# One low part per unit on GpSimd, a fourth raw buffer, and seven of eight groups with seven products

## The chip, the cores and the metric

The kernel runs on one core of a Trainium2 chip. The metric is the device time of one execution in microseconds (us); lower is better. TensorE (PE) multiplies, VectorE (DVE), ScalarE (ACT) and GpSimd (POOL) work on elements, SyncE (SP) issues the weight loads. Weights lie in HBM, tiles in SBUF, matmul results in the eight banks of PSUM.

## The reference

One decoder layer on 256 tokens of width 2048, in float32:

```
h = x + 0.5 * swiglu(rms_norm(x, g1), w_gate1, w_up1, w_down1)      # D_FF = 5632
h = h + mixer(rms_norm(h, gm))                                      # two groups of attention heads
y = h + 0.5 * swiglu(rms_norm(h, g2), w_gate2, w_up2, w_down2)
swiglu(x, g, u, d) = (silu(x @ g) * (x @ u)) @ d
```

The change concerns the two SwiGLU layers (FFN 1 up to about 705 us of the execution, FFN 2 from about 1044 us); the mixer between them is left as it is.

## The kernel before

**Products.** Every float32 weight tile is split into a high part (`hi`, rounded for TensorE, made by ACT from the loaded `raw` tile) and a low part (`lo` = `raw` - `hi`, a DVE subtraction of two SBUF tiles, called a low below; `low`, L440). One product (`product`, `mm3`) is three matmuls of 128 x 128 by 128 x 512: high by high, high by low, low by high.

**Groups.** A group is one 1 MB weight load: 128 partitions by four tiles of 512 columns, a 2 x 2 block of weight tiles against a 2 x 2 block of activation tiles (two halves of the contraction, two halves of the tokens). A group of kind `D` (`whole`, L443) does the eight products of a plain block product: one load, one ACT cast of 2048 columns, one low of 2048 columns. A group of kind `S` (`seven`, L480) does the same block with seven products in the manner of Winograd's form of Strassen's method. DVE first makes four sums of weight tiles (`outer`, L499: two at once; `inner`, L506 and L507: one after the other) in a `sums` tile, and then needs two lows, one of 1536 columns for the plain tiles and one of 2048 for the sums. The sums of the activation tiles (`form_of`, the tiles `fu`) are made once for each pair of contraction tiles, the first time that pair is used in an `S` group.

**Units.** A unit (`unit`) is 512 columns of gate and 512 of up, with eight groups, one for each pair of contraction tiles; `UNITS` gives the kind of each. An FFN has 11 units. When the last `S` group has ended, its banks `Q0` to `Q3`, which are common to the unit, are folded into the four results by eight DVE operations, the steps (`step`, L699): each reads one PSUM bank and one SBUF tile. Two SiLUs on ACT and two DVE multiplications (L722, the `s` tile, called f below) follow, then eight transposes on PE (L571) and their split into `hT` (again PSUM against SBUF). The down projection of unit b - 1, four `D` groups (`down`, `DOWN`), stands behind unit b's groups; the last two units' downs end the FFN.

**Order.** Nothing here is ordered by dependencies at run time alone: `arrange` walks through all tasks of an FFN with a cost for each (`cast`, `sub`, `LOADS`, a due place in PE's sequence, buffers taken and given back) and writes one fixed order for each engine. Every engine then works through its own list, waiting on semaphores. Buffers are counted in `NRAW` (loaded tiles), `NSUM`, `NHI` and `NLO`: 3, 2, 5 and 5. All weight loads are issued from the one SP queue, in the order of the groups.

Of the kernel before, what the change touches and what calls it, by code (L numbers as in the profile page):

```python
# [9 lines left out]
F32 = mybir.dt.float32  # L10
# [7 lines left out]
P = 128  # L18
# [77 lines left out]

class Task:
    def __init__(self, eng, cost, run, need=(), due=0, take=(), give=(), lag=LAG, rows=False, moves=0):
        self.moves, self.seeds = moves, None
        self.eng, self.cost, self.run, self.need, self.due = eng, cost, run, list(need), due  # L100
        self.take, self.give, self.lag, self.rows = dict(take), list(give), lag, rows
        self.got, self.end, self.then = {}, None, []


def arrange(tasks, pools):
# [19 lines left out]
    dirty = set(pools["bank"])  # L125
    queues, seen = {"sp": [], "pool": []}, [0.0]
# [30 lines left out]

    def open_(t):
        if t.seeds is not None and (takers[t.seeds] > takers[pos] or all(b in dirty for b in free["bank"])):
            return False  # L160
        return all(len(free[r]) >= k and (r not in lines or lines[r][0] is t) for r, k in t.take.items())
# [90 lines left out]
def hybrid_layer(ctx: ExitStack, tc: tile.TileContext, a: dict, out: bass.AP):  # L252
# [124 lines left out]
    def mm3(o, shi, slo, mhi, mlo, start, stop, seeded=False):  # L377
        nc.tensor.matmul(o, lhsT=shi, rhs=mhi, start=start, stop=False, skip_group_check=seeded)  # L378
        nc.tensor.matmul(o, lhsT=shi, rhs=mlo, start=False, stop=False, skip_group_check=seeded)  # L379
        nc.tensor.matmul(o, lhsT=slo, rhs=mhi, start=False, stop=stop, skip_group_check=seeded)  # L380
# [29 lines left out]
    def ffn(pool, u, wgu, wd, slots, banks, rstd, held=None, first=None, lead=None, done=None, out=None):  # L410
# [15 lines left out]
        def own(tag, i, shape, dt):  # L426
            if (tag, i) not in made:
                made[tag, i] = (sp if tag == "sqh" else pool).tile(shape, dt, tag=tag, name=tag, bufs={"s": 1}.get(tag, 2))
            return made[tag, i]
# [10 lines left out]
        def low(o_, a, b):  # L440
            tt(out=o_, in0=a, in1=f32(b), op=ALU.subtract)  # L441

        def whole(src, pieces):  # L443

            n, new, by = 2048 // pieces, [], []
            for j in range(pieces):
                m = slice(j * n, j * n + n)
                ld = task("sp", 0.06, None, take={"raw": 1} if j == 0 else (), lag=0, moves=1 / pieces)
                c = task("act", cast(n), None, [ld], take={"hi": 1} if j == 0 else ())
                l = task("dve", sub(n), None, [c], take={"lo": 1} if j == 0 else ())  # L450
# [7 lines left out]
                ld.run = lambda raw=raw, m=m: nc.sync.dma_start(raw(), src[:, m])  # L458
                c.run = lambda raw=raw, hi=hi: nc.scalar.copy(hi(), raw())  # L459
                l.run = lambda raw=raw, hi=hi, lo=lo: low(lo(), raw(), hi())  # L460
# [19 lines left out]
        def seven(src):  # L480
# [5 lines left out]
            b = task("dve", 2 * sub(512), None, [a])  # L486
# [17 lines left out]
            def inner():  # L504
                s, r = cols_of(sm()), cols_of(raw())
                tt(out=s[2], in0=s[0], in1=r[2], op=ALU.add)  # L506
                tt(out=s[3], in0=s[2], in1=r[1], op=ALU.add)  # L507

            a.run, b.run = outer, inner
            w = [([c, l], lambda i=i: (cols_of(hi())[i], cols_of(lo())[i])) for i in range(3)]  # L510
            w += [([cb, ls], lambda i=i: (cols_of(hs())[i], cols_of(lt())[i])) for i in range(4)]
            new = [(ld, -30), (c, 0), (a, 0), (l, 0)] + [(t, 3) for t in (ca, b, cb, ls)]
            return new, w, {2: [("hi", c), ("lo", l)], 6: [("hi", ca), ("lo", ls)]}

        def product(held, key, stat, w, need):
# [9 lines left out]
            def run():  # L525
                mm3(bank_of(b), *stat(), *w[1](), start=b["first"] is t, stop=b["last"] is t, seeded="seed" in b)
# [5 lines left out]
        def group(kind, src, held, stat, need, form=None, pieces=1, last=False):  # L532

            new, w, free = seven(src) if kind == "S" else added_low(src) if kind == "L" else whole(src, pieces)
# [46 lines left out]
        def into_u(un, gcol, due):  # L581

            def finish(k, v, x):
                ends = []
                for j in range(2):
# [4 lines left out]
                    ), [c] + ends[-1:], due)  # L590
# [33 lines left out]
        def form_of(p, need, due):  # L624

            tile_, over = fu[seven_of.index(p)], u(2 * p)[:, :, P:SEQ]
# [17 lines left out]
            def round_():  # L644
                x = views(a)[1]
                nc.scalar.copy(tile_[:, :, 0, :], x[:, :3])
                nc.scalar.copy(over[:, 0, :], x[:, 3])

            def left():
                x = views(a)[1]  # L650
                low(tile_[:, :, 1, :], x[:, :3], tile_[:, :, 0, :])
# [5 lines left out]
            at = lambda i: (tile_[:, i, 0, :], tile_[:, i, 1, :]) if i < 3 else (over[:, 0, :], over[:, 1, :])  # L657
# [4 lines left out]
        def unit(b):  # L662
# [29 lines left out]
            if ns:  # L692
# [4 lines left out]
                def step(o_, key, in1, op, need, due, free=True):  # L697
                    return task(
                        "dve", 0.605, lambda: tt(out=o_(), in0=bank_of(held[key]), in1=in1(), op=op), need + [held[key]["last"]], due,  # L699
                        give=[("bank", held[key]["first"])] if free else (),  # L700
                    )

                s0, s1 = lambda: s_tile()[:, 0, :], lambda: s_tile()[:, 1, :]
                d1 = step(x, "Q2", s0, ALU.add, [q], due)
                d2 = step(y, "Q1", x, ALU.subtract, [d1], due, False)
                d3 = step(s1, "Q3", x, ALU.add, [d1], due)
                d4 = step(x, "Q1", s1, ALU.subtract, [d2, d3], due)
                up = (y, x)
                g = [step(s0, (0, 0), s0, ALU.add, [d1], due + 1), step(s1, (1, 0), s1, ALU.add, [d3, d4], due + 4)]
                v = [step(y, (0, 1), y, ALU.add, [d2], due + 1), step(x, (1, 1), x, ALU.add, [d4], due + 5)]  # L710
            ends = []
            for t in range(NT):
# [8 lines left out]
                src = up[t] if ns else (lambda t=t: bank_of(R(t, 1)))  # L721
                f = task("dve", 0.66, lambda t=t, src=src: stt(  # L722
                    out=s_tile()[:, t, :], in0=src(), scalar=half_rms()[:, t : t + 1], in1=s_tile()[:, t, :], op0=ALU.mult, op1=ALU.mult,
                ), [a, v[t] if ns else R(t, 1)["last"]], due + 9 if ns else due + 2 * t, lag=1.5)
                if not ns:
                    f.give.append(("bank", R(t, 1)["first"]))
# [5 lines left out]
            def finish(k, v, x):  # L732
# [6 lines left out]
                l = task("dve", 0.605, lambda: low(rows_tile()[:, :, 1, :], v(), rows_tile()[:, :, 0, :]), [c], due + 4)  # L739
# [10 lines left out]
        rm_need, row_ready, row_of, row_split, moved = [], {}, {}, {}, {}  # L750

        def down(blocks, final):
# [5 lines left out]
            for i, (cp, b, c) in enumerate(todo):  # L758
# [4 lines left out]
                if not held[cp] and not final:  # L763
# [7 lines left out]
                    lambda k, b=b, c=c: row_ready[b, c], last=final_of_cp,  # L771
                )
# [11 lines left out]
        def settle(cp, held, final, later):  # L784

            due, ends = len(main), []
            for t in range(NT):
                for j in range(2):
                    tail = out is not None and cp == 1 and (t, j) == (1, 1)
                    for n, (a0, w) in enumerate(((0, 256), (256, 256)) if tail else ((0, 512),)):  # L790
# [11 lines left out]
                        x = task(*(("dve", sub(w)) if final else ("act", cast(w))), run, [held[t, j]["last"], *([moved[cp, t, j]] if final else [])], due + t + 4 * j, lag=0.6)  # L802
# [556 lines left out]
    with tc.tile_pool(name="f2", bufs=1, reuse_waits=REUSE) as fp:  # L1359
        slots, fu = [[], [], [], []], []  # L1360
        for i, nm, dt in F2_ORDER:
            if i == 4:
                fu += [fp.tile([P, 3, 2, P], F32R, name="fu%d" % p) for p in range(max(k.count("S") for k in UNITS[1]))]
            else:
                slots[i].append(fp.tile([P, 2048], dt, name="%s%d" % (nm, len(slots[i]))))
# [4 lines left out]
            lead={"residual": last_quarter, "next": (u2, ss2, V_G2), "forms": fu}, out=out.rearrange("(t p) d -> p t d", p=P),  # L1370
# [83 lines left out]
```

## Time and profile before

| what | value |
| --- | --- |
| time, median of 3 runs | 1744.66 us (1744.55 to 1745.9) |
| the profiled execution's own time | 1746.08 us |
| its span, first to last instruction | 1744.3 us |
| PE busy in the span | 1733.2 us (99%) |
| DVE busy | 1530.9 us (88%) |
| ACT busy | 1133.9 us (65%) |
| POOL busy | 11.5 us (1%) |
| granted TensorE clock | 1.00 |

A row of a timeline gives the start in us, the length in us, the engine, the line, the operation and its tiles, and in brackets the idle time of that engine ahead of it with what ended it. Operations of one engine overlap a little at their ends, so the time that one costs its engine is the distance from its start to the next one's. A row of busy times by stretches gives the stretch, its length, and for each engine the busy time and (x) the instructions.

### The profile page before, as it was taken

The numbers are of one execution on the slowest core, as the hardware profiler recorded it, in microseconds if no ns is written. First come the engines' busy times: TensorE is split into PE (matmuls) and PEld (weight loads), VectorE is DVE, ScalarE is ACT, GpSimd is POOL, SyncE is SP. The second block draws the span as 40 slices with busy tenths as digits, with TensorE's granted clock in tenths as the row PEclk, the third lists the DMA queues.
The fourth block names the chain that finished last, engine by engine and source line by source line (L and its number), as shares of the span: only waits on it lengthen the run. The fifth ranks groups of instructions, "written<-read, shape, count | busy, mean of one in ns | idle before, by whom it ended". The sixth has DMA issues, their size and how long they took to land.

```text
span 1744.3 us, 21098 instructions
## 1 busy us (share of the span) xinstructions
PE 1733.2 (99%) x8037; PEld 1440.2 (83%) x8037; DVE 1530.9 (88%) x1662; ACT 1133.9 (65%) x1380; POOL 11.5 (1%) x22
## 2 busy tenths in 40 slices
PE   9999999999999999999999999999999999999999
PEld 6888888888888888998788888888888888888887
DVE  7999999999999996668777769999999999999993
ACT  7677667767766764555766556667767766766761
POOL 0000000000000000000000000000000000000000
PEclk9999999999999999999999999999999999999999
DMA  8556556555545554564444456545555545555552
GB/s 340 197 206 224 201 185 217 196 190 217 216 175 212 217 208 154 157 206 158 133 146 144 133 185 249 181 181 219 192 193 217 210 178 216 217 202 185 218 195 118
DMA packets 62917, 339.73 MB, mean 195 GB/s; under 512 B 6752, under 2 KB 15456, under 8 KB 29280
## 3 DMA queue, kind: packets, MB, share of 16 engines
q1 hardware_dynamic: 62208, 337.18, 54.0%
q8 instruction: 63, 1.03, 0.2%
q0 software_dynamic: 320, 1.05, 0.1%
q14 instruction: 38, 0.31, 0.1%
q10 hardware_dynamic: 288, 0.16, 0.0%
HBM read 336.27 MB, written 2.10 MB: 194 GB/s over the span
## 4 chain that ended last, share of the span: by engine, by line
PE 95%; DVE 2%; ACT 1%; DMA 1%; issue 0%; SPq 0%; DVEq 0%; ACTq 0%
PE acc L379 24%; PE acc L378 24%; PE acc L380 24%; PE sm L378 6%; PE sm L379 6%; PE sm L380 6%; PE acc L571 1%; DVE wloy L441 1%; PE sm L1097 1%; PE sc L1286 1%; DMA rawx<-in_wgu 1%; PE sm L1103 1%; PE sm L1265 0%; DMA rawy<-in_wd 0%; DVE wlo L441 0%
## 5 line engine op out<-in xcount | busy, mean ns | idle before, releaser
L378 PE MATMUL acc<-whi,u 128*128 128x512 f32 (+1 forms) x671 | 256.1, 383 | 0.9 <-DVE s L1061 0.9
L379 PE MATMUL acc<-wlo,u 128*128 128x512 f32 (+1 forms) x671 | 256.2, 382 | 0.7 <-DVE wlo L441 0.6
L380 PE MATMUL acc<-whi,u 128*128 128x512 f32 (+1 forms) x671 | 254.7, 381 | 0.0
L295 DVE TENSOR_TENSOR wlo<-raw,whi 128x1024 fp32r<-128x1024 f32 (+1 forms) x112 | 128.8, 1154 | 70.4 <-ACT whi L294 69.8
L294 ACT CAST whi<-raw 128x1024 fp32r<-128x1024 f32 (+1 forms) x112 | 111.0, 991 | 93.2 <-PE acc L380 84.8
L441 DVE TENSOR_TENSOR wlo<-raw,whi 128x1536 fp32r<-128x1536 f32 (+3 forms) x76 | 146.7, 1934 | 6.6 <-ACT whi L459 6.5
L378 PEld LDWEIGHTS acc<-whi,u 128*128 128x128 f32 x671 | 125.9, 188 | 23.4 <-DVE s L1061 1.3
L379 PEld LDWEIGHTS acc<-wlo,u 128*128 128x128 f32 x671 | 126.0, 188 | 23.1 <-DVE wlo L441 2.0
L380 PEld LDWEIGHTS acc<-whi,u 128*128 128x128 f32 x671 | 125.8, 188 | 21.3 <-issue 0.8
L441 DVE TENSOR_TENSOR wlo<-sums,whi 128x2048 fp32r<-128x2048 f32 x46 | 105.1, 2285 | 16.2 <-ACT whi L487 16.2
L441 DVE TENSOR_TENSOR wlox<-raw,whix 128x2048 fp32r<-128x2048 f32 (+1 forms) x52 | 109.9, 2120 | 2.5 <-ACT whix L459 2.5
L441 DVE TENSOR_TENSOR wloy<-raw,whiy 128x1536 fp32r<-128x1536 f32 (+1 forms) x52 | 104.4, 2008 | 5.6 <-ACT whiy L459 5.5
L795 ACT COPY h<-acc 128x512 f32<-128x512 f32 (+1 forms) x117 | 64.1, 557 | 67.8 <-PE acc L380 67.4
L441 DVE TENSOR_TENSOR wloy<-sums,whiy 128x2048 fp32r<-128x2048 f32 x37 | 84.6, 2286 | 11.9 <-ACT whiy L487 11.9
L499 DVE TENSOR_TENSOR sums<-raw 128x1024 f32<-128x1024 f32 x77 | 93.6, 1217 | 0.0
L441 DVE TENSOR_TENSOR wlox<-sums,whix 128x2048 fp32r<-128x2048 f32 x34 | 77.7, 2285 | 13.7 <-ACT whix L487 13.7
L378 PE MATMUL acc<-whi,hT 128*128 128x512 f32 x224 | 88.5, 395 | 0.0
L379 PE MATMUL acc<-wlo,hT 128*128 128x512 f32 x224 | 87.3, 390 | 0.0
L380 PE MATMUL acc<-whi,hT 128*128 128x512 f32 x224 | 87.2, 389 | 0.0
L379 PE MATMUL acc<-wlox,u 128*128 128x512 f32 x216 | 84.2, 390 | 0.6 <-DVE wlox L441 0.6
L459 ACT CAST whi<-raw 128x2048 fp32r<-128x2048 f32 (+2 forms) x42 | 73.2, 1747 | 17.5 <-DMA raw<-in_wd 11.2
L378 PE MATMUL acc<-whix,u 128*128 128x512 f32 x216 | 84.1, 389 | 0.0
(341 smaller groups left out, 4558.0 us busy)
## 6 DMA issues: line engine op xcount, KB each, us to landing
raw<-in_wgu SPq DMA_DIRECT2D x109, 1024.0 KB, 4.8
raw<-in_wd SPq DMA_DIRECT2D x65, 1024.0 KB, 4.9
rawy<-in_wgu SPq DMA_DIRECT2D x33, 1024.0 KB, 4.7
rawx<-in_wgu SPq DMA_DIRECT2D x32, 1024.0 KB, 5.0
raw<-in_wf SPq DMA_DIRECT2D x48, 512.0 KB, 3.6
raw<-in_wo SPq DMA_DIRECT2D x32, 512.0 KB, 3.3
raw<-in_ws SPq DMA_DIRECT2D x32, 388.0 KB, 3.5
rawx<-in_wd SPq DMA_DIRECT2D x12, 1024.0 KB, 4.8
```

Source lines behind the costliest of these rows:

```text
L294: nc.scalar.copy(hi, src)
L295: nc.vector.tensor_tensor(out=lo, in0=src, in1=hi.bitcast(F32), op=ALU.subtract)
L378: nc.tensor.matmul(o, lhsT=shi, rhs=mhi, start=start, stop=False, skip_group_check=seeded)
L379: nc.tensor.matmul(o, lhsT=shi, rhs=mlo, start=False, stop=False, skip_group_check=seeded)
L380: nc.tensor.matmul(o, lhsT=slo, rhs=mhi, start=False, stop=stop, skip_group_check=seeded)
L441: tt(out=o_, in0=a, in1=f32(b), op=ALU.subtract)
L459: c.run = lambda raw=raw, hi=hi: nc.scalar.copy(hi(), raw())
L499: tt(out=sm()[:, :1024].rearrange("p (j n) -> p j n", j=2), in0=v[:, 0:3:2, :], in1=v[:, 3:4, :].broadcast_to([P, 2, 512]), op=ALU.add,)
L571: nc.tensor.transpose(bt[:, j * SEQ + t * P : j * SEQ + (t + 1) * P], src()[:, t, m], ident)
L795: nc.scalar.copy(o_, src)
L1097: nc.tensor.transpose(bt[:, j * P : (j + 1) * P], src[:, j, :], ident)
L1103: nc.tensor.matmul(bo[rows, c0 : c0 + SEQ], lhsT=vals(0, j), rhs=p0[:, j, :], start=True, stop=False)
```

## The change

- `UNITS`: from the fourth unit on, `SDSSSSSD` becomes `SSSSSSSD`, in eight units of each FFN.
- `BESIDE`, `AT_Q2`, `low`, `whole`, `slow`: of each down that isn't the FFN's last, the second of its four groups gets its low from GpSimd instead of DVE. The GpSimd instruction is tied by a semaphore to the matmul that ends bank `Q2` of the unit in front, the same matmul that the first step waits for.
- `Task.pair`, `shared`: the planner doesn't put a DVE task without a PSUM operand and a GpSimd task into the same time.
- `step`: the two steps that make the up results write into the PSUM bank that they read, and f reads that bank; so f too reads one PSUM and one SBUF tile, and frees the bank.
- `NRAW` 3 to 4; to make room, `s` and `fu` tiles, `PAD` and `SCRATCH` (the memory set aside for descriptors of GpSimd's DMAs) are re-arranged or cut.
- `inner` becomes two tasks, so that other work can stand between L506 and L507 (now both L538).
- The rule for the copies of `h` into PSUM banks ahead of a down (`open_`, `seeds`) counts free banks.

```diff
-UNITS = [["D" * 8, x, "DSSSSSSD"] + ["SDSSSSSD"] * (NB - 3) for x in ("DDSSDSSD", "DSSDSSSD")]
+UNITS = [["D" * 8, x, "DSSSSSSD"] + ["SSSSSSSD"] * (NB - 3) for x in ("DDSSDSSD", "DSSDSSSD")]
 DOWN = "DDDD"
+BESIDE = (1,)
+AT_Q2 = True
-NRAW, NSUM, NHI, NLO = 3, 2, 5, 5
-SCRATCH = 2048
+NRAW = 4
+SCRATCH = 512
...
+def slow(n):
+    return 0.4 + 0.0021 * n
...
+    def shared(t):
+        x = doing.get({"dve": "pool", "pool": "dve"}.get(t.eng))
+        return t.pair and x is not None and x.pair and x.end is not None and x.end > now + 1e-9
...
-        def low(o_, a, b):
-            tt(out=o_, in0=a, in1=f32(b), op=ALU.subtract)
+        def low(o_, a, b, behind=None):
+            if behind is None:
+                tt(out=o_, in0=a, in1=f32(b), op=ALU.subtract)
+                return
+            x = nc.gpsimd.tensor_tensor(out=o_, in0=a, in1=f32(b), op=ALU.subtract)
+            tc.add_manual_dep(x.ins, behind.made.ins.name, ...
...
-            b = task("dve", 2 * sub(512), None, [a])
+            b0 = task("dve", sub(512), None, [a])
+            b = task("dve", sub(512), None, [b0])
...
-                v = [step(y, (0, 1), y, ALU.add, [d2], due + 1), step(x, (1, 1), x, ALU.add, [d4], due + 5)]
+                up = [lambda t=t: bank_of(held[t, 1]) for t in range(NT)]
+                v = [step(up[0], (0, 1), y, ALU.add, [d2], due + 1, False), step(up[1], (1, 1), x, ALU.add, [d4], due + 5, False)]
...
+                    behind=beside.get(b + 1) if not final and i in BESIDE else None,
```

**DVE at the end of a unit.** The rows are from the middle of FFN 1, from the last lows ahead of the steps to the second f. `wlo`, `wlox` are low tiles, `whi`, `whix` high tiles, `raw`, `rawx` loaded ones; `sqh` and `s` hold the folded results, `acc` and `sm` are PSUM banks. Before:

```order
L441 TENSOR_TENSOR wlo_75<-raw_70,whi_73 128x2048
L441 TENSOR_TENSOR wlox_93<-raw_71,whix_90 128x2048
L441 TENSOR_TENSOR wlox_94<-rawx_87,whix_91 128x2048
L699 TENSOR_TENSOR sqh<-sm,s 128x512
L699 TENSOR_TENSOR sqh<-acc,sqh 128x512
L699 TENSOR_TENSOR s<-sm,sqh 128x512
L699 TENSOR_TENSOR s<-acc,s 128x512
L699 TENSOR_TENSOR sqh<-acc,s 128x512
L699 TENSOR_TENSOR sqh<-acc,sqh 128x512
L699 TENSOR_TENSOR s<-acc,s 128x512
L722 SCALAR_TENSOR_TENSOR s<-sqh,rmh,s 128x512
L699 TENSOR_TENSOR sqh<-acc,sqh 128x512
```

Now, in the same place:

```order
L464 TENSOR_TENSOR wlox_95<-rawx_88,whix_92 128x2048
L464 TENSOR_TENSOR wlox_96<-raw_70,whix_93 128x2048
L733 TENSOR_TENSOR sqh<-acc,s 128x512
L733 TENSOR_TENSOR sqh<-acc,sqh 128x512
L733 TENSOR_TENSOR s<-sm,sqh 128x512
L733 TENSOR_TENSOR s<-acc,s 128x512
L733 TENSOR_TENSOR sqh<-acc,s 128x512
L733 TENSOR_TENSOR acc<-acc,sqh 128x512
L757 SCALAR_TENSOR_TENSOR s<-acc,rmh,s 128x512
L733 TENSOR_TENSOR s<-acc,s 128x512
L464 TENSOR_TENSOR wlo_75<-rawx_87,whi_73 128x2048
L733 TENSOR_TENSOR acc<-acc,sqh 128x512
```

One low fewer stands ahead of the steps (that of the second down group, now on GpSimd), the first eight operations from the first step on all read PSUM, and the first operation with two SBUF inputs (`wlo_75`) comes behind them; a second such low and the second f come next.

**DVE at the beginning of a unit's groups**, with the splits of the first group, still in FFN 1. Before, behind the `hT` splits, an `S` group's sums, a `D` group's low (`wlox_94<-raw_70`) and the next `S` group:

```order
L499 TENSOR_TENSOR sums_89<-raw_71 128x1024
L506 TENSOR_TENSOR sums_89<-sums_89,raw_71 128x512
L507 TENSOR_TENSOR sums_89<-sums_89,raw_71 128x512
L441 TENSOR_TENSOR wlox_94<-raw_70,whix_91 128x2048
L499 TENSOR_TENSOR sums_88<-rawx_87 128x1024
L506 TENSOR_TENSOR sums_88<-sums_88,rawx_87 128x512
L507 TENSOR_TENSOR sums_88<-sums_88,rawx_87 128x512
L441 TENSOR_TENSOR wlox_95<-raw_71,whix_92 128x1536
```

Now, from the second f on:

```order
L531 TENSOR_TENSOR sums_89<-raw_70 128x1024
L531 TENSOR_TENSOR sums_90<-raw_71 128x1024
L538 TENSOR_TENSOR sums_89<-sums_89,raw_70 128x512
L538 TENSOR_TENSOR sums_90<-sums_90,raw_71 128x512
L464 TENSOR_TENSOR hT<-acc,hT 128x2x256
L538 TENSOR_TENSOR sums_89<-sums_89,raw_70 128x512
L464 TENSOR_TENSOR hT<-acc,hT 128x2x256
L464 TENSOR_TENSOR wlox_95<-raw_70,whix_92 128x1536
L464 TENSOR_TENSOR wlox_96<-sums_89,whix_93 128x2048
L538 TENSOR_TENSOR sums_90<-sums_90,raw_71 128x512
```

The `D` group has gone from among the `S` groups, and the sums of two groups are made with other work between their single steps.

**GpSimd in FFN 1**, where it had nothing before the mixer; these are the first of nine such rows (FFN 2 has nine more):

```order
L466 ISA
L466 TENSOR_TENSOR wlo_75<-raw_71,whi_73 128x2048
L466 TENSOR_TENSOR wlox_96<-raw_71,whix_93 128x2048
L466 TENSOR_TENSOR wlox_95<-raw_71,whix_92 128x2048
L466 TENSOR_TENSOR wlox_94<-raw_71,whix_91 128x2048
```

All nine read `raw_71`, so that buffer's next load waits for GpSimd and no longer for DVE.

More of the change, by code (lines that the diff above doesn't have):

```diff
@@ L94, in sub, with __init__ @@
     return 0.07 + 0.00104 * n
+def slow(n):
+    return 0.4 + 0.0021 * n
 class Task:
-    def __init__(self, eng, cost, run, need=(), due=0, take=(), give=(), lag=LAG, rows=False, moves=0):
+    def __init__(self, eng, cost, run, need=(), due=0, take=(), give=(), lag=LAG, rows=False, moves=0, psum=False):
         self.moves, self.seeds = moves, None
+        self.pair = (eng == "dve" and not psum) or (eng == "pool" and not moves)
         self.eng, self.cost, self.run, self.need, self.due = eng, cost, run, list(need), due
@@ L156, in since @@
         return max([x.end + x.lag for x in t.need], default=0.0)
+    def shared(t):
+        x = doing.get({"dve": "pool", "pool": "dve"}.get(t.eng))
+        return t.pair and x is not None and x.pair and x.end is not None and x.end > now + 1e-9
     def open_(t):
-        if t.seeds is not None and (takers[t.seeds] > takers[pos] or all(b in dirty for b in free["bank"])):
+        if shared(t):
             return False
+        if t.seeds is not None:
+            left = len(free["bank"]) - (takers[t.seeds] - takers[pos])
+            if left < 1 or sum(b not in dirty for b in free["bank"]) < 1:
+                return False
         return all(len(free[r]) >= k and (r not in lines or lines[r][0] is t) for r, k in t.take.items())
@@ L449, in whole @@
                 c = task("act", cast(n), None, [ld], take={"hi": 1} if j == 0 else ())
-                l = task("dve", sub(n), None, [c], take={"lo": 1} if j == 0 else ())
+                l = task(*(("dve", sub(n)) if behind is None else ("pool", slow(n))), None, [c], take={"lo": 1} if j == 0 else ())
+                if behind is not None:
+                    l.need.append(behind)
                 if j == 0:
@@ L459, in whole @@
                 c.run = lambda raw=raw, hi=hi: nc.scalar.copy(hi(), raw())
-                l.run = lambda raw=raw, hi=hi, lo=lo: low(lo(), raw(), hi())
+                l.run = lambda raw=raw, hi=hi, lo=lo: low(lo(), raw(), hi(), behind)
                 new += [(ld, -30), (c, 0), (l, 0)]
@@ L525, in run @@
             def run():
-                mm3(bank_of(b), *stat(), *w[1](), start=b["first"] is t, stop=b["last"] is t, seeded="seed" in b)
+                t.made = mm3(bank_of(b), *stat(), *w[1](), start=b["first"] is t, stop=b["last"] is t, seeded="seed" in b)
             t.run = run
@@ L530, in product, with group @@
             return t
-        def group(kind, src, held, stat, need, form=None, pieces=1, last=False):
-            new, w, free = seven(src) if kind == "S" else added_low(src) if kind == "L" else whole(src, pieces)
+        def group(kind, src, held, stat, need, form=None, pieces=1, last=False, behind=None):
+            new, w, free = seven(src) if kind == "S" else added_low(src) if kind == "L" else whole(src, pieces, behind)
             n0 = len(main)
@@ L624, in form_of, with tile_ @@
         def form_of(p, need, due):
-            tile_, over = fu[seven_of.index(p)], u(2 * p)[:, :, P:SEQ]
+            over = u(2 * p)[:, :, P:SEQ]
+            def tile_():
+                return own("fu%d" % seven_of.index(p), 0, [P, 3, 2, P], F32R)
             def views(a):
@@ L697, in step @@
                 def step(o_, key, in1, op, need, due, free=True):
[L698 to L701, printed above, removed]
+                    x = task("dve", 0.605, None, need + [held[key]["last"]], due, give=[("bank", held[key]["first"])] if free else (), psum=True)
+                    x.run = lambda: setattr(x, "made", tt(out=o_(), in0=bank_of(held[key]), in1=in1(), op=op))
+                    return x
+                beside[b] = held["Q2"]["last"] if AT_Q2 else None
                 s0, s1 = lambda: s_tile()[:, 0, :], lambda: s_tile()[:, 1, :]
                 d1 = step(x, "Q2", s0, ALU.add, [q], due)
+                beside[b] = beside[b] or d1
                 d2 = step(y, "Q1", x, ALU.subtract, [d1], due, False)
@@ L800, in run @@
                                 q.dma_start(out[:, t, c : c + w], o_)
[L802 removed]
+                        x = task(*(("dve", sub(w)) if final else ("act", cast(w))), run, [held[t, j]["last"], *([moved[cp, t, j]] if final else [])], due + t + 4 * j, lag=0.6, psum=True)
                     x.give.append(("bank", held[t, j]["first"]))
```

63 lines of the change are left out of this document (33 added, 30 removed).

## The prediction

> **What bounds the kernel now.** I read the chain that ended last first, then PE's waits, then busy time by unit.
>
> ```profile
> PE 95%; DVE 2%; ACT 1%; DMA 1%; issue 0%; SPq 0%; DVEq 0%; ACTq 0%
> ```
> ```profile
> PE acc L379 <- DVE wlox L441: 0.6, 1, 0.6
> PE acc L571 <- ACT h L795: 0.6, 1, 0.6
> ```
> ```profile
> 104.30:167.77 63.47, 62.85 (x279) 51.35 (x279) 63.09 (x67) 44.30 (x50) 0.00 (x0) 1.00 0.52 197
> 291.80:353.97 62.17, 62.17 (x280) 51.49 (x279) 58.86 (x49) 43.14 (x47) 0.00 (x0) 1.00 0.56 204
> ...
> 540.39:602.54 62.15, 62.15 (x279) 51.47 (x279) 58.85 (x49) 43.04 (x47) 0.00 (x0) 1.00 0.55 203
> ```
>
> PE is the bound; the two single waits of 0.6 us are among the longest it has. The last rows are units with their downs, PE, PEld, DVE, ACT and POOL in that order: five steady ones (two shown) take 62.13 to 62.17 us, all of it PE. DVE is busy for 58.85 us of each, so it has 3.3 us to spare. The first row is an early unit in which DVE had almost nothing to spare (63.09 of 63.47): there PE lost 0.62 us, no more.
>
> **PE: what goes.** A steady unit has 6 x 7 + 2 x 8 + 4 x 8 = 90 products, or 270 matmuls, and eight transposes.
>
> ```profile
> 352.00 0.39 PE L380 MATMUL sm<-whix,hT 128*128 128x512 f32 x1
> 352.23 0.60 PE L571 MATMUL acc<-cst,s 128*128 128x128 f32 x4
> 352.59 0.48 PE L378 MATMUL sm<-whix,hT 128*128 128x512 f32 x1
> ```
>
> A matmul costs 0.23 us from start to start, not the 0.39 of its own length. Four transposes cost 352.59 - 352.23 = 0.36 us, eight 0.72; (62.15 - 0.72) / 90 = 0.68 us a product. Eight units in each of two FFNs lose one product: 16 x 0.68 = 10.9 us less. A changed unit with its down takes 61.47 us, if PE never waits.
>
> **DVE: does it still fit?** One `S` group:
>
> ```profile
> 307.39 2.29 DVE L441 TENSOR_TENSOR wlox<-sums,whix 128x2048 fp32r<-128x2048 f32 x1 [2.67 <-ACT whix L487]
> ...
> 311.27 1.22 DVE L499 TENSOR_TENSOR sums<-raw 128x1024 f32<-128x1024 f32 x1
> 312.41 2.29 DVE L441 TENSOR_TENSOR wlox<-sums,whix 128x2048 fp32r<-128x2048 f32 x1
> 314.61 0.68 DVE L506 TENSOR_TENSOR sums<-sums,raw 128x512 f32<-128x512 f32 x1
> 315.33 0.69 DVE L507 TENSOR_TENSOR sums<-sums,raw 128x512 f32<-128x512 f32 x1
> 315.94 1.22 DVE L499 TENSOR_TENSOR sums<-raw 128x1024 f32<-128x1024 f32 x1
> 317.07 1.75 DVE L441 TENSOR_TENSOR wlo<-raw,whi 128x1536 fp32r<-128x1536 f32 x1
> 318.74 0.68 DVE L506 TENSOR_TENSOR sums<-sums,raw 128x512 f32<-128x512 f32 x1
> ```
>
> From start to start: sums 1.14 + 0.72 + 0.61, lows 1.67 + 2.20, together 6.3 us. A `D` group is one low, 2.2. A changed unit swaps a `D` for an `S` (+4.1) and gives one low to GpSimd (-2.2): 58.85 + 1.9 = 60.75 us of 61.47. The single steps save up to 0.11 each where other work now stands between L506 and L507 (0.72 against 0.61), in four of seven groups, 0.4 at most; I don't count it. So DVE fits, with 0.7 us to spare instead of 3.3. Its longest wait in that unit (2.67) is behind an ACT cast; PE lost nothing by it, so there DVE was merely ahead, and I take such waits as free to vanish.
>
> ```profile
> 329.73 1.91 ACT L459 CAST whi<-raw 128x2048 fp32r<-128x2048 f32 x1
> ...
> 334.75 0.59 ACT L695 COPY s<-acc 128x512 f32<-128x512 f32 x1 [1.29 <-PE acc L380]
> ```
>
> ACT's casts grow from 2048 to 3584 columns in the swapped group, some 1.4 us at 1.91 for 2048, to 44.6 of 61.47 us: hidden.
>
> **The new GpSimd low and the steps beside it.**
>
> ```profile
> 896.08 1.29 POOL L364 TENSOR_TENSOR sss<-sss,sqh 128x512 f32<-128x512 f32 x1 [13.72 <-ACT sqh L363]
> ```
> ```profile
> 896.97 1.48 DVE L295 TENSOR_TENSOR wlo<-raw,whi 128x1024 fp32r<-128x1024 f32 x1 [0.81 <-ACT whi L294]
> 899.37 1.23 DVE L295 TENSOR_TENSOR wlo<-raw,whi 128x1024 fp32r<-128x1024 f32 x1 [0.91 <-ACT whi L294]
> ```
> ```profile
> 339.50 0.68 DVE L699 TENSOR_TENSOR sqh<-sm,s 128x512 f32<-128x512 f32 x1
> 340.21 0.69 DVE L699 TENSOR_TENSOR sqh<-acc,sqh 128x512 f32<-128x512 f32 x1
> 340.82 0.68 DVE L699 TENSOR_TENSOR s<-sm,sqh 128x512 f32<-128x512 f32 x1
> ...
> 343.82 0.75 DVE L722 SCALAR_TENSOR_TENSOR s<-sqh,rmh,s 128x512 f32<-128x512 f32 x1
> ```
>
> GpSimd needs 1.29 us for 512 columns. The trace has no 2048. Four times as much is 5.2; if part of it is fixed, as on DVE (0.61 for 512 columns, 2.20 for 2048, 3.6 times), it is 4.65, and by ACT's copies (0.59 and 1.91, 3.2 times) 4.2. I take 4.65, the engine with the same operation. [...]
>
> The DVE rows show the danger: the low that began at 896.97, while GpSimd worked until 897.37, took 1.48 us and not 1.23. It stood until GpSimd was done. [...]
>
> The place, counted from the end of `Q2`: one product ends the `S` group and eight end the last `D` group, results (0,0), (0,1), (1,0), (1,1) after 3, 5, 7 and 9 products, 2.0, 3.4, 4.8 and 6.1 us. DVE does three steps, the fourth and the first result as they come, f, and then waits for (1,0) at 4.8: this step ends at about 5.5, and the next operation is a low with two SBUF inputs. GpSimd starts at about 0.1 and ends at 4.75, at most at 5.3. It fits, by 0.2 to 0.75 us. If DVE is late with its lows, as above (PE came to the transposes, 21 products behind `Q2`, at 352.23, so `Q2` was done at 337.9; the first step began at 339.50, with no idle time ahead), GpSimd is held too, and the eight operations behind take 5.1 us at 0.6 to 0.7 each without any wait, which covers 4.65. So I put the collisions at 0 (bounds 0 and 0.3 a unit). PE wants this low one `D` group later, at 6.1 + 5.4 = 11.5: hidden. The second f, now behind two lows, ends at 5.5 + 2.2 + 0.6 + 2.2 + 0.7 = 11.2; PE comes to the transposes 8 + 3 products into the downs, at 13.6. If that cover of 2.4 us is gone, PE waits, product by product. SP's next load into `raw_71` now waits for GpSimd, until 4.8; DVE reads it behind the second f and one sum, at 12.4, and a load takes 4.8 us (below); the load behind it in the queue waits for a low that ends at 7.7 anyway.
>
> **The other edits.** The pair that becomes `S` needs its activation sums once in each FFN:
>
> ```profile
> 20.15 0.76 DVE L637 TENSOR_TENSOR sqh<-u 128x256 f32<-128x256 f32 x2
> 21.88 0.48 DVE L913 SCALAR_TENSOR_TENSOR u<-xs,vec,u 128x256 fp32r<-128x256 f32 x1
> ...
> 24.88 0.55 DVE L441 TENSOR_TENSOR fu<-sqh,fu 128x384 fp32r<-128x384 f32 x1
> 25.34 0.28 DVE L441 TENSOR_TENSOR u<-sqh,u 128x128 fp32r<-128x128 f32 x1
> ```
>
> 1.73 + 0.67 = 2.4 us, which puts DVE at 63.15 in a unit of 61.47, 1.7 over. Buffered lows cover part; the early unit above, as full, cost PE 0.62. Bounds 0 and 1.7; I take 0.5 twice, +1.0. The fourth raw buffer lets the fourth big load go out before DVE frees the first buffer:
>
> ```profile
> 5.55 0.51 SPq L458 DMA_DIRECT2D rawx<-in_wgu  x1
> ...
> 9.81 0.33 SPq L458 DMA_DIRECT2D raw<-in_wgu  x1
> ```
> ```profile
> raw<-in_wgu SPq DMA_DIRECT2D x109, 1024.0 KB, 4.8
> ```
> ```profile
> 1724.88 0.54 POOL L800 DMA_DIRECT2D out<-h  x1 [0.82 <-DVE h L797]
> ```
>
> The load of 5.55 is the one that PE's 0.6 us wait on `wlox` hangs on. If the two share the bandwidth, it lands later by at most a load's own 4.8 us; if the queue serves them in turn, by nothing, and I take 0, since PE already lost only 0.6 there with every load of the start under way. Less memory for the descriptors of GpSimd's four output DMAs, the last issued at 1724.88, can cost only what exceeds the 19 us to the end: 0. A GpSimd low in units that had no spare DVE time may save the 0.6 at `h`; not counted.
>
> **The sum.** Against the profiled execution (span 1744.3, 1746.1 by its own time): 1746.1 - 10.9 + 1.0 = 1736.2. The median of the runs lies 1.4 lower, so 1734.8.
>
> **The rivals.**
> - DVE becomes the bound. 0.7 us to spare is less than the 3.3 that it waits now. If 1 us a unit of those waits stays, a unit takes 61.75 and the 14 full units give back 4; if 2 stay, 62.75 and 18. Times 1738.7 to 1752.7; against it, that PE's waits in the steady units are nil, and that the fourth raw buffer and the single steps loosen DVE. At 1.4 us a unit nothing is left of the gain.
> - The slower one: the steps are held as well, or GpSimd starts so late (behind its ACT cast or its buffer) that the lows behind the steps are. Each unit then pays up to 4.65 us on DVE: 60.75 + 4.65 = 65.4, 3.9 over PE, 14 units 55 us: about 1790. It decides from 1.4 us a unit on. [...]
> - The start pays for the fourth buffer: up to 4.8 us, 1739.6.
>
> **How the numbers follow.** PE stays the bound 0.68; start 0.07; DVE the bound 0.15 (0.06 faster, 0.06 same, 0.03 slower); held steps 0.10. A measurement of this kernel tells 0.2%, 3.5 us, from nothing. Faster 0.81, same 0.06, slower 0.13. Low end: no new waits and the old 0.6 and 0.6 gone, 1732.6, so 1732; high end 1744, which leaves out the held steps and the worse half of the DVE case.
>
> **What would show it.** PE's row of a steady unit at 61.5 us with PE busy throughout; DVE at 60 to 61 in it; GpSimd at 4.2 to 5.2 us, starting within 0.2 us of the end of `Q2`, with steps of 0.68 beside it and the low behind them at 2.29, not longer. Wrong if steps grow beyond 0.7, if lows of 4 us and more follow them, or if PE waits for `wlo` or at L602 in every unit.

## The result, and the profile after

The changed kernel takes 1733.88 us (median of 6 runs, 1733.76 to 1734.49) against 1745.09 us for the kernel before on the same chip: a ratio of 0.9937, 95% interval 0.9926 to 0.9948. The prediction was 1734.8 us. The profiled execution took 1734.49 us, with a span of 1732.7 us, 11.6 less than before.

First the busy times of the kernel before, then those of the changed kernel with the shares of the chain that ended last, then PE's two longest waits at the weight products, both at the start:

```profile
PE 1733.2 (99%) x8037; PEld 1440.2 (83%) x8037; DVE 1530.9 (88%) x1662; ACT 1133.9 (65%) x1380; POOL 11.5 (1%) x22
```
```profile
PE 1721.5 (99%) x7989; PEld 1431.7 (83%) x7989; DVE 1557.7 (90%) x1724; ACT 1161.1 (67%) x1416; POOL 106.7 (6%) x40
...
PE 97%; DVE 1%; DMA 1%; ACT 1%; SPq 0%; issue 0%; DVEq 0%; ACTq 0%
```
```profile
PE acc L401 <- DVE wlo L464: 0.8, 1, 0.8
PE acc L401 <- DVE wlox L464: 0.5, 1, 0.5
```

PE is still the bound, now with 97% of the chain, and it makes 8037 - 7989 = 48 matmul instructions fewer: 16 products of three. Busy times by unit (stretch, length, then PE, PEld, DVE, ACT and POOL), two early units and a steady one:

```profile
104.60:166.80 62.20, 62.20 (x280) 51.47 (x279) 61.35 (x66) 43.82 (x49) 4.65 (x1) 1.00 0.55 199
166.80:228.80 62.00, 61.74 (x277) 50.78 (x276) 60.99 (x58) 45.22 (x49) 6.60 (x1) 1.00 0.55 197
...
349.19:410.60 61.41, 61.41 (x277) 50.94 (x276) 60.50 (x52) 44.76 (x48) 5.20 (x1) 1.00 0.58 206
```

A steady unit lasts 61.41 us, all of it PE; DVE is busy for 60.50 of it, ACT for 44.8. Where the 11.6 us went is seen from the transposes that end FFN 1 and the first ones of FFN 2, before (L571):

```profile
683.55 1.91 PE L571 MATMUL acc<-cst,h 128*128 128x128 f32 x16
...
1053.81 0.75 PE L571 MATMUL acc<-cst,h 128*128 128x128 f32 x4
```

and after (L602):

```profile
677.39 0.60 PE L602 MATMUL acc<-cst,h 128*128 128x128 f32 x4
...
1047.65 0.76 PE L602 MATMUL acc<-cst,h 128*128 128x128 f32 x4
```

FFN 1 gave 6.16 us and the mixer nothing. The rest, 11.6 - 6.16 = 5.44, is FFN 2: eight products at 0.68. FFN 1 has 0.7 beyond its eight products. It is a balance: PE's wait in the early unit of before (0.62 in its row) is gone, one of 0.26 has come in the next unit, and the start and the transposes have changed a little; the part on the prediction adds them up.

The end of a unit in FFN 1, on GpSimd (a unit in the middle, and the first one, where DVE had no low in hand) and on DVE in that middle unit:

```profile
397.13 5.20 POOL L466 TENSOR_TENSOR wlo<-raw,whi 128x2048 fp32r<-128x2048 f32 x1 [56.22 <-PE acc L402]
...
88.61 4.63 POOL L466 TENSOR_TENSOR wlo<-raw,whi 128x2048 fp32r<-128x2048 f32 x1 [88.16 <-PE acc L402]
```
```profile
395.55 2.28 DVE L464 TENSOR_TENSOR wlox<-raw,whix 128x2048 fp32r<-128x2048 f32 x1
397.75 0.69 DVE L733 TENSOR_TENSOR sqh<-acc,s 128x512 f32<-128x512 f32 x1
398.47 0.69 DVE L733 TENSOR_TENSOR sqh<-acc,sqh 128x512 f32<-128x512 f32 x1
...
401.67 0.75 DVE L757 SCALAR_TENSOR_TENSOR s<-acc,rmh,s 128x512 f32<-128x512 f32 x1
402.33 0.68 DVE L733 TENSOR_TENSOR s<-acc,s 128x512 f32<-128x512 f32 x1
402.93 2.28 DVE L464 TENSOR_TENSOR wlo<-rawx,whi 128x2048 fp32r<-128x2048 f32 x1
```

GpSimd is released at 397.13 by the end of `Q2`, while DVE's last low still runs, until 397.83. Its row is 5.20 us long; with no low of DVE ahead of it (88.61) the same low takes 4.63. So it stood for 0.57 us behind DVE's low and then worked until 402.33. The seven PSUM operations beside it take 0.68 to 0.75 us, as they did alone in the kernel before, the eighth begins as it ends, and the next low with two SBUF inputs begins at 402.93, free by 0.6 us, at its full speed of 2.28.

### The profile page after: what moved, and what is told of

It reads as the page before. It is cut to its first block, busy times and chain, and to the rows that moved or that the text cites. A ratio compares the mean times of both kernels' runs of the same rounds, so it can differ in the third digit from the quotient of the medians.

```text
span 1732.7 us, 21114 instructions
## 1 busy us (share of the span) xinstructions
PE 1721.5 (99%) x7989; PEld 1431.7 (83%) x7989; DVE 1557.7 (90%) x1724; ACT 1161.1 (67%) x1416; POOL 106.7 (6%) x40
## 4 chain that ended last, share of the span: by engine, by line
PE 97%; DVE 1%; DMA 1%; ACT 1%; SPq 0%; issue 0%; DVEq 0%; ACTq 0%
PE acc L401 25%; PE acc L400 25%; PE acc L402 25%; PE sm L401 6%; PE sm L402 6%; PE sm L400 6%; PE acc L602 1%; PE sm L1131 1%; PE sc L1320 1%; DMA rawx<-in_wgu 1%; PE sm L1137 1%; PE sm L602 0%; PE sm L1299 0%; DVE wloy L464 0%; PE sc L1245 0%; PE sm L1138 0%
## 5 line engine op out<-in xcount | busy, mean ns | idle before, releaser
L400 PE MATMUL acc<-whi,u 128*128 128x512 f32 (+1 forms) x659 | 251.5, 383 | 1.1 <-DVE s L1095 0.9
L402 PE MATMUL acc<-whi,u 128*128 128x512 f32 (+1 forms) x659 | 249.9, 381 | 0.0
L464 DVE TENSOR_TENSOR wlo<-sums,whi 128x2048 fp32r<-128x2048 f32 x53 | 121.2, 2287 | 3.2 <-ACT whi L519 2.3
L464 DVE TENSOR_TENSOR wlo<-raw,whi 128x1536 fp32r<-128x1536 f32 (+3 forms) x57 | 107.3, 1884 | 8.1 <-ACT whi L490 7.1
L464 DVE TENSOR_TENSOR wloy<-sums,whiy 128x2048 fp32r<-128x2048 f32 x41 | 93.7, 2286 | 2.4 <-ACT whiy L519 1.7
L464 DVE TENSOR_TENSOR wlox<-rawx,whix 128x2048 fp32r<-128x2048 f32 (+1 forms) x42 | 86.4, 2058 | 6.2 <-ACT whix L490 5.1
L464 DVE TENSOR_TENSOR wlox<-sums,whix 128x2048 fp32r<-128x2048 f32 x39 | 89.2, 2286 | 0.7
L538 DVE TENSOR_TENSOR sums<-sums,raw 128x512 f32<-128x512 f32 x130 | 87.8, 687 | 1.3
L400 PE MATMUL acc<-whi,hT 128*128 128x512 f32 x216 | 84.8, 392 | 0.0
L402 PE MATMUL acc<-whi,hT 128*128 128x512 f32 x216 | 84.1, 389 | 0.0
L464 DVE TENSOR_TENSOR wloy<-raw,whiy 128x2048 fp32r<-128x2048 f32 (+1 forms) x39 | 80.1, 2053 | 3.7 <-ACT whiy L514 1.8
L401 PE MATMUL acc<-wloy,u 128*128 128x512 f32 x205 | 80.0, 390 | 0.4 <-DVE wloy L464 0.3
```

What stands on the lines that cost most here:

```text
L402: return nc.tensor.matmul(o, lhsT=slo, rhs=mhi, start=False, stop=stop, skip_group_check=seeded)
L538: tt(out=s[n + 2], in0=s[2 * n], in1=cols_of(raw())[r], op=ALU.add)
```

## The experiments

Theory: PE's 16 products are the whole gain, and everything else is there so that DVE can keep up with the shorter unit. Rivals: the other edits take or give time by themselves; DVE is the bound; the steps are held by GpSimd, or are free for another reason than their PSUM operand. Each expectation was written before its run; unless said otherwise a kernel is the changed one with the edit shown, timed against the kernel before. PEld is PE's weight load.

**e1_old_units: the change without its fewer products.**

```diff
-... ["DSSSSSSD"] + ["SSSSSSSD"] * (NB - 3) ...
+... ["DSSSSSSD"] + ["SDSSSSSD"] * (NB - 3) ...
```

> The changed kernel with the old kinds of groups (SDSSSSSD), all other edits kept. If the gain is the 16 products that PE no longer does, it all goes: a unit back at 62.15 us, 1733.9 + 10.9 = 1744.8 us. If the other edits (GpSimd low, fourth raw buffer, single steps) carry part of it, 1735 to 1741.

Measured: 1745.0 us, ratio 1.0001 (0.9992 to 1.0011). A unit is back at its old length, with GpSimd at work and DVE at only 56.86:

```profile
350.28:412.44 62.16, 62.16 (x280) 51.39 (x279) 56.86 (x48) 43.20 (x46) 4.64 (x1) 1.00 0.55 202
```

The other edits together neither give nor take anything that can be measured while PE has 90 products a unit.

**e2_no_gpsimd: every low on DVE again.**

```diff
-BESIDE = (1,)
+BESIDE = ()
```

> The changed kernel with all lows on VectorE. If VectorE's 60.5 us of a 61.4 us unit leave only 0.9 to spare, 2.2 more make it the bound: 62.7 to 63.3 us in each of 14 units, 1752 to 1760 us, slower than the kernel before. If the GpSimd low isn't needed (VectorE has slack that its busy time hides), 1734 to 1736.

Measured: 1747.22 us, ratio 1.0014 (1.0004 to 1.0023).

```profile
477.24:539.27 62.03, 62.03 (x277) 50.63 (x276) 61.96 (x53) 44.84 (x47) 0.00 (x0) 1.00 0.56 207
```

DVE fills the unit (61.96 of 62.03) and is the bound. PE's busy time reads 62.03 too, though as many instructions take it 61.41 in the changed kernel: short waits don't show in it. The direction was right and the size wrong: one low of 2.20 us more on DVE made its busy time 1.46 longer, not 2.2. The 60.50 of the changed kernel is not all needed work. It holds small stalls where an operation follows the one that it reads: in the changed kernel, two dependent single sums, and two that belong to different groups,

```profile
421.14 1.41 DVE L538 TENSOR_TENSOR sums<-sums,rawx 128x512 f32<-128x512 f32 x2
422.47 2.28 DVE L464 TENSOR_TENSOR wlo<-sums,whi 128x2048 fp32r<-128x2048 f32 x1
...
438.71 1.29 DVE L538 TENSOR_TENSOR sums<-sums,raw 128x512 f32<-128x512 f32 x2
439.91 1.75 DVE L464 TENSOR_TENSOR wlo<-raw,whi 128x1536 fp32r<-128x1536 f32 x1
```

cost 1.33 and 1.20 us from start to the next one's start. With DVE behind and more work in hand, the planner parts all but one of e2's seven pairs in that unit; the changed kernel leaves three together, 0.26 of the 0.74 that is missing. The rest are like delays between other operations: added up over the unit, the distances from one start to the next exceed the shortest one of each kind of operation by 1.9 us in the changed kernel (0.9 idle, 1.0 counted as busy) and by 0.3 in e2.

**e3_low_at_once: GpSimd's low as soon as its data are there, not tied to `Q2`.**

```diff
-        if shared(t):
-            return False
...
-            tc.add_manual_dep(x.ins, behind.made.ins.name, ...)
...
-                    l.need.append(behind)
```

> The GpSimd low no longer waits for the end of bank Q2 and the planner no longer keeps it apart from VectorE: it begins when its high part is there, among VectorE's lows. If the two engines shut each other out whenever both have two SBUF inputs, VectorE loses up to 4.6 us a unit, 0.9 of it hidden: 14 x 3.7 = 52, up to 1786 us, with single lows of 4 to 7 us beside a GpSimd low. If they only share, each some per cent slower, 1734 to 1740.

Measured: 1826.83 us, ratio 1.0469 (1.0452 to 1.0487). GpSimd and DVE, around the steps of one unit:

```profile
485.12 5.12 POOL L464 TENSOR_TENSOR wlox<-raw,whix 128x2048 fp32r<-128x2048 f32 x1 [60.95 <-ACT whix L482]
```
```profile
483.47 2.28 DVE L462 TENSOR_TENSOR wlox<-rawx,whix 128x2048 fp32r<-128x2048 f32 x1
485.67 6.72 DVE L462 TENSOR_TENSOR wlox<-raw,whix 128x2048 fp32r<-128x2048 f32 x1
492.31 0.68 DVE L725 TENSOR_TENSOR sqh<-acc,s 128x512 f32<-128x512 f32 x1
```

The low that meets GpSimd's takes 6.72 us and not 2.28: it is held for 4.44, almost GpSimd's whole work, and the steps behind it come late. Two units of it (the number ahead of the last two is the granted clock):

```profile
419.04:485.12 66.08, 62.20 (x276) 50.67 (x275) 64.75 (x52) 44.74 (x48) 5.12 (x2) 1.00 0.53 191
485.12:552.81 67.69, 63.85 (x276) 51.80 (x275) 64.82 (x52) 44.70 (x48) 5.12 (x1) 0.97 0.51 187
```

Over the eighteen lows the loss against the changed kernel is 93 us, 5.2 each. The first of these units is 66.08 - 61.41 = 4.67 us longer, more than DVE's stall: none of DVE's 0.9 us of idle time absorbed it. The stall stands on the path from `Q2` over the steps and f to the transposes, where PE then waits for DVE (1.96 us at 441.55); and DVE's own wait in the unit grows to 0.96 us, for an ACT cast behind copies of `h` that wait for PE in turn. That, and eighteen lows where fourteen were counted, is why this is dearer than the 1786 us at most that was expected. The edit takes out both the semaphore and the planner's rule that keeps the two engines apart; no run parts them. The second is longer by another 1.6, of which more below (the granted clock is 0.97).

**e4_three_raw: the old number of loaded tiles** (`NRAW = 4` to `3`).

> Three raw buffers instead of four, all else kept. Twelve loads a unit in 61.4 us are one each 5.1 us, so three buffers allow 15.4 us from issue to release; a load takes 4.8 and the GpSimd group's stays until 5 us behind Q2. If the 0.9 us that VectorE has to spare cover the later loads, 1734 to 1737; if the fourth buffer is needed to feed VectorE, waits for DMA of about 1 us a unit or more, 1745 and above. The start shows the other side: without the fourth load PE's first waits should be shorter by up to 0.3 us.

Measured: 1735.04 us, ratio 0.9944 (0.9929 to 0.9959), not to be told from the changed kernel's 0.9937. As long as GpSimd takes its low, the fourth buffer isn't needed. At the start PE waits only 0.2 us at the weight products in this run, and the first transposes of FFN 1 come at 56.98 us, against 58.17 in the changed kernel. But that time differs as much among kernels with the same number of buffers: 56.98 to 58.08 us in the five profiles with three (before, e4, e7, e9, e11), 57.29 to 58.17 in the eight with four. A cost of the fourth buffer at the start can't be told from that.

**e5_sums_together: the sums of a group in one task of two steps, as before.**

```diff
-            b0 = task("dve", sub(512), None, [a])
-            b = task("dve", sub(512), None, [b0])
+            b = task("dve", 2 * sub(512), None, [a])
```

> The changed kernel with the two single sums as one task again, one behind the other. Each pair then costs VectorE 1.33 us instead of 1.20. Four of seven pairs in a unit are affected, 0.5 us; VectorE has 0.9 us idle in a unit of 61.4 and waits of its own of some 0.7 besides, so PE stays the bound: 1733.5 to 1735. If the single steps were needed to make it fit, units of 61.6 to 62 and 1737 to 1742.

Measured: 1737.97 us, ratio 0.9964 (0.9951 to 0.9977): 4 us above the changed kernel, a miss of the case that I held likelier. Units are 0.2 longer:

```profile
335.86:397.45 61.59, 61.59 (x277) 50.82 (x276) 60.75 (x52) 44.70 (x48) 5.29 (x1) 1.00 0.58 205
```

DVE still has 0.84 us without work, and yet PE is slower. Where PE loses is seen at the transposes. In the changed kernel all eight stand in one stretch; here they stand in two, nine matmuls apart (the last row is the weight load of the second four):

```profile
410.44 1.03 PE L602 MATMUL acc<-cst,s 128*128 128x128 f32 x8
```
```profile
349.17 0.60 PE L601 MATMUL sm<-cst,s 128*128 128x128 f32 x4
```
```profile
351.73 0.42 PEld L601 LDWEIGHTS sm<-cst,s 128*128 128x128 f32 x4 [0.31 <-DVE hT L464]
```

The second four wait for DVE's split of the first into `hT`. They do so in 14 units of e5, and never in the changed kernel. Counted from start to start, with 0.2267 us for every matmul of a product, a unit's transposes cost PE 0.89 us in the changed kernel and 1.07 here: that is the whole 0.18.

I had taken idle time for reserve, and I read the loss as DVE's: its idle time lies ahead of a stretch without any gap (370.87 to the first step at 398.15) and can't take up what the pairs add in it, and the chain that ended last goes over DVE for 9% of the span, against 1%. But in this unit the chain stays on PE, and e1, with DVE busy for only 56.86 us, has the same two stretches and a wait between them:

```profile
414.73 0.43 PEld L602 LDWEIGHTS acc<-cst,s 128*128 128x128 f32 x4 [0.20 <-DVE hT L464]
```

There want of DVE time can't be the reason. So the order that the planner finds has its part in the loss, and how much of the 4 us is DVE's time isn't shown.

**e6_up_in_sbuf: the up results in SBUF again, so that f has two SBUF inputs.**

```diff
-                up = [lambda t=t: bank_of(held[t, 1]) for t in range(NT)]
+                up = (y, x)
```

> The changed kernel with the up results written to SBUF as before, so that f has two SBUF inputs. The first f begins 0.6 to 0.7 us before the GpSimd low ends: if two SBUF inputs are what shuts an operation out, this f and only it becomes longer, 1.3 to 1.5 us instead of 0.75, the steps stay at 0.69, and the 0.66 us go into VectorE's 0.9 of idle time: 1733.5 to 1735. If f isn't held, it stays at 0.75.

Measured: 1734.8 us, ratio 0.9945 (0.993 to 0.996). GpSimd's low, and the first f and the step behind it on DVE:

```profile
396.78 5.19 POOL L466 TENSOR_TENSOR wlo<-raw,whi 128x2048 fp32r<-128x2048 f32 x1 [56.27 <-PE acc L402]
```
```profile
401.30 1.23 DVE L757 SCALAR_TENSOR_TENSOR s<-sqh,rmh,s 128x512 f32<-128x512 f32 x1
402.45 0.68 DVE L733 TENSOR_TENSOR s<-acc,s 128x512 f32<-128x512 f32 x1
```

GpSimd ends at 401.97. f, now with two SBUF inputs, takes 1.23 us and not 0.75; the steps ahead of it, with one PSUM input, take 0.68 to 0.69 and are not held, and the second f (408.05), behind the end of GpSimd's low, takes 0.74. So for f the operand is what decides. Its price, 0.5 us from start to start, hardly reaches the end of the unit.

**e7_units_alone: the kernel before with the new `UNITS` and nothing else.**

> The kernel before with the new kinds of groups (SSSSSSSD) alone: three raw buffers, all lows on VectorE, the sums together. If VectorE's work sets the unit, it is 62.0 us (all lows on VectorE in the changed kernel) plus up to 0.9 for the sums, 62.0 to 62.9: 1746 to 1760 us, no gain though PE has 48 matmuls less. If PE's work alone counts, 1734 to 1736.

Measured: 1775.53 us, ratio 1.0178 (1.0161 to 1.0195): 31 us slower than before, twice the loss that I expected at most.

```profile
486.25:550.22 63.97, 62.58 (x277) 50.52 (x276) 62.84 (x53) 44.06 (x48) 0.00 (x0) 1.00 0.55 199
```

DVE is the bound, with 0.9 us more of busy time than in e2 and, besides, 1.1 us without work. Which edit is missed, e9 to e11 ask.

**e8_two_lows: a second low of each down on GpSimd** (`BESIDE = (1,)` to `(1, 2)`).

> Two lows of each down on GpSimd (second and third group) instead of one. The steps cover only the first: the second runs from about 4.7 to 9.3 us behind bank Q2, and the first VectorE low behind the steps is held until then, 2 to 4 us longer than 2.29. VectorE has 2.2 us less to do, so that it comes out even, and PE stays the bound: 1733 to 1738. If GpSimd's work beside VectorE's lows were free, no low would be longer than 2.3 us and VectorE's busy time in a unit would be 58.3; the time would still be 1734.

Measured: 1735.16 us, ratio 0.9947 (0.9932 to 0.9962).

```profile
396.85 5.21 POOL L466 TENSOR_TENSOR wlo<-raw,whi 128x2048 fp32r<-128x2048 f32 x1 [51.30 <-PE acc L402]
402.00 4.67 POOL L466 TENSOR_TENSOR wlo<-rawx,whi 128x2048 fp32r<-128x2048 f32 x1
```
```profile
404.47 4.34 DVE L464 TENSOR_TENSOR wlox<-rawx,whix 128x2048 fp32r<-128x2048 f32 x1
```

GpSimd's second low runs until 406.67, past the PSUM operations, and DVE's low is held for 2.06 us: what the offload frees (2.2) the hold takes back.

**e9, e10, e11: no GpSimd low, with three raw buffers, with the sums together, and with both.** The edits are those of e2, e4 and e5.

> The changed kernel without the GpSimd low and with three raw buffers. It asks which of the other edits carry the 28 us between e2 (all lows on DVE, 1747.2) and e7 (only UNITS changed, 1775.5). Theory A, the fourth raw buffer matters once DVE is the bound, because with three a load, and so an ACT cast, is late for DVE now and then (e7's DVE stood 1.2 us a unit waiting for casts): units of about 63.2 instead of 62.03, 14 to 16 of them, 1762 to 1767. Theory B, it matters no more than with GpSimd (e4: 1.2 us): 1747 to 1750, units of 62.0 to 62.2.

> The changed kernel without the GpSimd low and with the sums again in one task of two steps, four raw buffers kept. With DVE the bound, the dependent pair (1.33 us from start to start, 1.20 with other work between its steps) costs 0.12 in each of seven groups, 0.85 us a unit: units of about 62.9, 14 to 16 of them, 1759 to 1761. If the single steps also spare DVE a wait for casts, more, up to e7's 64.1 and 1775; if most pairs can't be parted anyway, 1748 to 1752.

> Both at once: no GpSimd low, three raw buffers, sums in one task. If buffers and sums make up the whole of e7's loss, 1772 to 1777 with units of about 64. If something else in the change does (f reading PSUM, the rule for the copies of h), it stays at 1760 to 1768.

Measured: e9 1751.53 us, ratio 1.0035 (1.0022 to 1.0048); e10 1774.63, 1.0171 (1.0156 to 1.0186); e11 1776.49, 1.0185 (1.0168 to 1.0202). So nearly all of what e7 loses against e2 comes with the paired sums; the fourth buffer is worth 4.3 us with DVE as the bound, between the two theories, and e11 already has e7's time, so the other edits (f's operand, the rule for the copies of `h`) have no share in it that can be seen. One unit of e10 and places on DVE in it:

```profile
484.49:548.29 63.80, 62.48 (x276) 50.63 (x275) 62.66 (x53) 44.23 (x48) 0.00 (x0) 1.00 0.55 200
```
```profile
513.47 2.74 DVE L537 TENSOR_TENSOR sums<-sums,raw 128x512 f32<-128x512 f32 x4
516.12 1.75 DVE L464 TENSOR_TENSOR wlo<-raw,whi 128x1536 fp32r<-128x1536 f32 x1
...
526.45 1.75 DVE L464 TENSOR_TENSOR wlox<-rawx,whix 128x1536 fp32r<-128x1536 f32 x1
529.03 2.29 DVE L464 TENSOR_TENSOR wlo<-sums,whi 128x2048 fp32r<-128x2048 f32 x1 [0.83 <-ACT whi L518]
```

Four dependent sums take 2.65 us to the next start, and none of the seven pairs is parted, where e2 leaves one: 6 x 0.13 = 0.8 us. And DVE stands 0.83 for an ACT cast, which it does not in e2's unit. Together 1.6 of the 63.80 - 62.03 = 1.77. What makes the cast late there was not tried.

GpSimd's low and the single steps are thus two ways to the same room on DVE, and the second one is worth much only where the first is missing. The theory put it too widely: beside these two, the fourth buffer (e4) and f's operand (e6) can't be told from nothing, and the rule for the copies of `h` was not tried with GpSimd's low.

| all with the new `UNITS`, four raw buffers | single steps | sums together |
| --- | --- | --- |
| one low a unit on GpSimd | 1733.88 us | 1737.97 us |
| all lows on DVE | 1747.22 us | 1774.63 us |

## Why the prediction was right

- **16 products at 0.68, PE the bound.** Shown: a steady unit is 0.74 shorter, and e1, without the fewer products, gave nothing (1.0001). A unit was to last 61.47 us if PE never waits; it lasts 61.41.
- **DVE fits.** Predicted 60.75 of 61.47, measured 60.50 of 61.41. That its 3.3 us of waits could shrink freely to less than one held. How much was left to spare isn't known: e5, without the single steps that the prediction didn't count, adds 0.25 us of busy time and PE pays 0.18, at the transposes, with the planner's order as a rival cause. The rival "DVE becomes the bound" is real one edit further: e2 and e7 are it.
- **GpSimd's low.** Taken as 4.65 us (4.2 to 5.2), by DVE's scaling from 512 columns; measured 4.63. That it would be held by a late low of DVE came true (0.57), and so did the cover: the first low behind the PSUM operations was free by 0.6, predicted 0.2 to 0.75. The second f ends at 408.67, 1.8 us ahead of the transposes (410.44); predicted were 2.4.
- **Collisions at nothing.** The term stood on the PSUM operand and on the place behind `Q2`. No row of the kernel before has a step beside a GpSimd operation, so that the steps would go on was my assumption; in the changed kernel the PSUM operations beside GpSimd take 0.68 to 0.75 us. Both supports were tested: f with two SBUF inputs is held (1.23 us, e6), a low on DVE that meets GpSimd is held for up to 4.44 us (e3).
- **The activation sums of the added pair, +1.0 us.** The sum's one loss is there, 0.5 us in the unit of each FFN in which the new sums are made (at 174.77 and 1157.64; in FFN 2 that unit still has six `S` groups):

```profile
209.96 0.39 PE L400 MATMUL sm<-whi,u 128*128 128x512 f32 x1
210.60 0.50 PE L401 MATMUL sm<-wlo,u 128*128 128x512 f32 x1 [0.26 <-DVE wlo L464]
210.94 0.40 PE L402 MATMUL sm<-whi,u 128*128 128x512 f32 x1
```
```profile
1183.88 0.39 PE L400 MATMUL acc<-whiy,u 128*128 128x512 f32 x1
1184.56 0.50 PE L401 MATMUL acc<-wloy,u 128*128 128x512 f32 x1 [0.29 <-DVE wloy L464]
```

From start to start 0.64 and 0.34 us in FFN 1, 0.68 and 0.34 in FFN 2, where a matmul takes 0.23: some 0.5 us each, twice what the bracket says. PE waits like this in no later unit. That it is the new sums that make DVE late there was not tried by a run of its own. There is another candidate: the two lows that PE waits for had themselves stood for an ACT cast, 0.83 us until 208.26 and 1.67 until 1182.22, so ACT's order may be what made them late. If so, the term had the right size by luck.
- **Mis-sized: the waits of before.** The forecast left them in place. PE's wait of 0.62 at the transposes of the early unit was 0.8 from start to start, with 0.2 more at the transposes ahead of it; both are gone. FFN 2 lost one of 0.2. Transposes wait like this, for a copy of `h` by ACT, in e7, e9 and e11 too (5.6, 5.2 and 2.1 us in all, weight loads included), which like the kernel before have three raw buffers and all lows on DVE; the profiles with the fourth buffer or GpSimd's low have 0.6 us of it at most. What links them wasn't tried. And sixteen units are 0.06 shorter than worked out, at most 1.0: most of it because the eight transposes now stand in one stretch and cost 0.89 us, where the two stretches of before (352.23 and 353.37) cost 0.93 to 0.96. Against these, the first transposes of FFN 1 come 0.24 us later (58.17 against 57.93). For FFN 1 that makes 8 x 0.68 + 1.0 + 8 x 0.06 - 0.5 - 0.24 = 6.2 us, and 6.16 were measured. Together these cover the 1.7 us by which the profiled execution beat its forecast (1734.49 against 1736.2). The median beat its own by 0.9 only, since this profiled execution lay 0.6 above the median and the one before 1.4: that the number came so near is in part luck.
- **Fourth raw buffer at nothing** at the start: neither shown nor refuted. The runs agree within what they can tell (e4), and the first transposes vary by 1 us among the profiles.
- **The slower rival** (the lows behind the steps are held) was put at about 1790 us. e3 made a collision of this kind, with the low ahead of the steps, at 1826.83: such a low is held (6.72 us and not 2.28), and that is dearer than I had priced it. I had let DVE's idle time absorb part of it and counted 14 units, and in some units of e3 PE is slow for a while behind its wait (0.42 to 0.43 us a matmul and not 0.23). That the steps themselves are held showed in no run.

## What to carry to other kernels

In this kernel the low given to GpSimd belongs beside VectorE operations that read PSUM (0.68 to 0.75 us there, as alone), and it has to be held back until they come: a second low on GpSimd meets an SBUF-to-SBUF operation, which takes 4.34 us and not 2.28, and gains nothing (e8), and lows that start at once cost 93 us (e3). When a change makes the bound engine's stage shorter, don't take the other engine's idle or busy time in that stage for its reserve: it depends on where that engine must wait, and its busy time holds small stalls (in e2 a low of 2.20 us more made it 1.46 longer). Test each enabling edit alone and with the others missing: the single steps are worth 4 us or 27, depending on the rest. And look at the bound engine's own rows, its weight loads too, before a loss is put down to another engine: an edit here also changes the order that the planner finds (e5).

## What was unexpected in the hardware

In e3 PE stands for almost 2 us at the transposes, and what follows is slow. Timeline rows, and then the chain's pieces (start, length) from there:

```profile
507.62 0.66 PE L594 MATMUL acc<-cst,s 128*128 128x128 f32 x4 [1.94 <-DVE hT L462]
508.04 0.48 PE L398 MATMUL acc<-whix,hT 128*128 128x512 f32 x1
```
```profile
508.89 0.42 PE acc L400
...
511.45 0.43 PE sm L400
511.87 0.28 PE acc L398
512.15 0.23 PE acc L399
```

From 508.89 to 511.87, 3.0 us, a matmul costs 0.42 to 0.43 us from start to start, with one partly slow on either side (0.37 at 508.51, 0.28 at 511.87), and then 0.23 again. Of the units of FFN 1 some show this and some don't, behind gaps of the same length (behind 1.96 us at 441.55 the matmuls go on at 0.23); where it comes the unit's granted clock is 0.97, and it is 1.6 us longer. At 0.20 us lost in each 0.43 that makes some 3.4 us of slow work, an estimate from these rows. Why PE is slow behind some of these gaps and not behind others, no run shows. So a DVE stall that makes PE wait can cost more than its own length: in the unit of 485.12 one of 4.44 us made it 67.69 - 61.41 = 6.28 longer; the steady units of the changed kernel have no such gap.

The other thing is small: a DVE operation of 512 columns behind the one that it reads begins 0.12 us later than behind an independent one (1.33 against 1.20 us for a pair). At six pairs a unit in 16 units, with DVE as the bound, that is an estimated 12 of the 27 us between e2 and e10.
